# Gate products of a recurrent layer as one fp32 matmul, with a new transfer model in the kernel's order generator

## The chip, the cores and the metric

The program runs on one core of a Trainium2 chip. The metric is device microseconds (us) of one execution of the whole program; the time given for a kernel is the median of several runs. One further execution was recorded by the hardware profiler, and all durations, waits and idle times below come from that record.

The core has four compute engines with a queue of instructions each, and each queue is worked off in order: PE (matrix products), DVE (vector work), ACT (activation functions and copies) and POOL (general work). SP is the fifth queue; here it issues all DMA transfers. An engine whose next instruction has to wait holds everything behind it.

## The reference

Two layers over a sequence of 2048 frames of width 1024, batch 1, all in fp32. Layer 0 is a recurrent block, layer 1 a gated delta rule. Cut to what the change touches, layer 0 is

```
cond = silu(c) @ ada_w + ada_b                     # shift, scale, gate of each layer
h    = rmsnorm(x) * (1 + scale) + shift
xb, zg = split(h @ in_w)                           # 1024 -> 2 x 1024
xf   = causal_conv4(xb) + conv_b
pre  = einsum('bsni,knij->kbsnj', xf, gate_w)      # 2 gates, 8 blocks of 128 x 128
r, i = sigmoid(pre + gate_b)
a    = exp(-8 * r * softplus(-lam))
hseq = scan(a, sqrt(1 - a*a) * (i * xf))           # linear recurrence over time
x    = x + gate * ((hseq * silu(zg)) @ out_w)
```

The line `pre` holds the gate products. Layer 1 projects to q, k, v, z and two small columns, convolves, runs the delta rule in chunks for 8 heads of 128, and projects back; a final rmsnorm follows.

## The kernel before, in words

Time runs along the free dimension in tiles of 128 partitions by 512 columns. The sequence is done in two halves (`u`, 1024 frames each) of two tiles (`i`). PE's main work are the projections ("mm" for the input projections, "mmo" for the output projections, both at line 696): every fp32 operand is split into a high and a low part of the rounded type fp32r, and each product is three matmuls, high by high, low by high and high by low. The splits cost a cast and a subtraction on ACT, DVE or POOL.

The stages follow one another: the conditioning vector (0 to 60 us); the input projection of layer 0 with convolution, gates and scan (about 60 to 500); its output projection out1 with the normalisation and transposition of what layer 1 reads (500 to 700); the projections and heads of layer 1 (700 to 1700, and some of it later); out2 and the final norm (to 1914).

The gates of layer 0: `conv1_thread` produces xf (three multiply-adds on DVE at line 786, which read the product from PSUM, and a few small steps that end at line 799). `gates_thread` makes its high part xh (ACT, line 828) and its low part xl (DVE, line 831). `lru_thread` loads the gate weights gw and splits them into gh (ACT, line 902) and gl (POOL, line 905). For each of the two gates three matmuls follow (line 837), then `gate_thread` applies the activation. `z1_thread` makes the gate path tz (ACT line 813, DVE line 815). The normalised input of the second half is split into hh and hl by `split_thread` (DVE lines 596 and 598), after it was stored transposed and loaded again (xt_d, stored at line 537, loaded as xk at line 573). In out1, `y_thread` loads yf (line 951) and splits it into yh (ACT, line 955) and yl (DVE, line 959).

No order of instructions is written out. Threads (Python generators) ask for an engine and a duration, `Weave` plays them against its own clock and writes the instructions down in the order in which it reaches them. So every number in a `yield`, and every rule in `Weave.transfer`, sets the order on all five queues; it does not change what an instruction costs. `transfer` says when a planned transfer has landed; `MARGIN` is a reserve behind landings: a thread that uses loaded data waits a half or the whole of it (in the plan alone) before it asks for an engine. On the chip, the semaphores between the engines make every instruction wait for what it really needs.

Of the kernel before, what the change touches and what calls it, by code (L numbers as in the profile page):

```python
# [16 lines left out]
P = 128  # L17
# [3 lines left out]
TC = 512  # L21
# [11 lines left out]
MARGIN = 2.4  # L33
# [7 lines left out]
LANDS = {"sp": 1.375, "st": 1.07}  # L41
# [32 lines left out]
class Weave:  # L74
    def __init__(self):
# [3 lines left out]
        self.landed = [0.0] * 8  # L79
# [21 lines left out]
    def start(self, th):  # L101
# [9 lines left out]
        if w[0] in LANDS:  # L111
            return max(th.t, self.free["sp"], self.landed[-8])
# [17 lines left out]
    def transfer(self, th, t, kind, dur, wait=True):  # L130

        self.free["sp"] = t + 0.45
        self.free["dma"] = max(t + 1.04, self.free["dma"]) + dur
        self.landed.append(self.free["dma"] + LANDS[kind])
        th.t = self.landed[-1] + 0.05 if wait else t + 0.45

    def run(self):
        while self.threads:
# [15 lines left out]
            elif w[0] in LANDS:  # L154
# [9 lines left out]
def trunk_kernel(ctx, tc, x, head, small, ada_w, ada_b, final_g, w1, gate_w, ow1, w2, wab, ow2, out):  # L164
# [17 lines left out]
    def f(ap):  # L182
        return ap.bitcast(F32)
# [45 lines left out]
    tags |= {t: ("l1", n) for t, n in {"xh": 2, "xf1": 2, "tg": 4, "th": 2, "tz": 2, "gw": 1, "gh": 1, "gl": 1, "head": 1}.items()}  # L229
# [79 lines left out]
    def first_loads_thread():  # L309

        yield ev("firstpanel")
        for half in range(2):
# [19 lines left out]
    def first_small_thread():  # L332
        yield "sp", 0.29, False
        sp.dma_start(out=head_s, in_=head)
        w.spawn(arrive_thread(ev("head")), 0)
        yield "sp", 0.29, False
# [82 lines left out]
    def row_halves_thread(parts):  # L419
# [3 lines left out]
        for layer, part, d in parts:  # L423
            ttok = yield slots["tt"]
            acc = tile_([P, TC], "tt", "acc")
            for q in range(4):
                wtok = yield slots["raw"]
                yield "sp", 1.4
# [27 lines left out]
            yield "sp", 1  # L456
# [6 lines left out]
            if layer == 1:  # L463
                yield "st", 0.29
# [60 lines left out]
    def turn_thread(key, t_d, xt, tok, ttok, b):  # L525
        yield from scale_thread(xt, ev("scaled", key, b), True)
        for d in range(2):
# [7 lines left out]
            for c_ in range(4):  # L535
                yield "st", 0.31, c_ == 3
# [86 lines left out]
    def panel_load(name, p):  # L623
# [3 lines left out]
        yield "sp", 1.4, False  # L627
# [5 lines left out]
    def panels_thread():  # L633
        yield ev("small")
        ahead = []
        for name, panels, _ in plans:
            for m, p in enumerate(panels):
# [23 lines left out]
                if name[1] > 0:  # L661

                    kept = yield ev("kept", p)
                    yield "sp", 1.4, False
# [18 lines left out]
    def keep_thread(p, lo):  # L683
        kept = dram.tile([P, KT, P], F32, name=f"wlo_d{p[0]}{p[1]}{p[2]}")
        yield "st", 1.4
# [133 lines left out]
    def gates_thread(u, n, i):  # L819
        xf, ftok = yield ev("xf", u, n, i)  # L820
        gh, gl = yield ev("gw", u, n)
        etok = yield slots["xh"]
        ltok = yield slots["xr"]
        if (u, n, i) == (NU - 1, KT - 1, NTC - 1):
            w.set(ev("lasthalves"))
        yield "act", 0.521
        xh = tile_([P, TC], "xh", "xh", F32R)
        act.copy(xh, xf)
        yield "dve2", 0.599
        xl = tile_([P, TC], "xr", "xl", F32R)  # L830
        dve.tensor_tensor(xl, xf, f(xh), ALU.subtract)
        for g in range(2):
            ctok = yield slots["c"]
            yield "pe", 0.696
            pg = ps.tile([P, TC], F32, tag="c", name="pg")
            for q, (a, b) in enumerate(((gh, xh), (gh, xl), (gl, xh))):
                pe.matmul(pg, lhsT=a[:, g, :], rhs=b, start=(q == 0), stop=(q == 2))
            w.spawn(gate_thread(u, n, i, g, pg, ctok), 3)
        put("xh", etok)
        put("xr", ltok)  # L840
# [36 lines left out]
        yield "st", 1  # L877
# [13 lines left out]
    def lru_thread():  # L891
        for u in range(NU):
            for n in range(KT):
                wtok = yield slots["gw"]
                yield "sp", 0.48
                gw = tile_([P, 2, P], "gw", "gw")
                sp.dma_start(out=gw, in_=gate_w[n])
                htok = yield slots["gh"]
                ltok = yield slots["gl"]
                yield "act", 0.302  # L900
                gh = tile_([P, 2, P], "gh", "gh", F32R)
# [901 lines left out]
```

## Time and profile before

| | us |
|---|---|
| median of 3 runs | 1911.61 |
| the runs | 1911.36 to 1918.54 |
| profiled execution, its own time | 1915.63 |
| span in its record, first to last instruction | 1913.9 |
| mean granted TensorE clock | 0.988 of full speed |

In the views, "busy" of PE is counted from modelled ends of pipelined matmuls: two matmuls that follow each other at 0.23 us are drawn 0.39 us long each. What a matmul costs in a stream is therefore the distance from its start to the next start. "Idle before" and the waits are gaps in which PE had nothing in flight. A wait is written as "engine line it stood at <- what ended the wait".

### The profile page before, as it was taken

The page shows a single profiled execution, that of the slowest core. Times are in us where ns is not written, and L with a number is a line of the kernel's source. Part 1 is how long each engine was busy: PE and PEld are TensorE (multiplying, and loading weights), DVE is VectorE, ACT ScalarE, POOL GpSimd, SP SyncE. Part 2 cuts the span into 40 slices and gives each one's busy share as a digit, 9 for nine tenths or more (in the row PEclk, how much of TensorE's full clock was granted, in tenths as well). Part 3 has the DMA queues.
Part 4 walks back from the last instruction along what each step waited for, and adds up shares of the span by engine and source line. Part 5 has one row for each costly group of instructions (what it writes and reads, how often), then busy time and mean ns, then how long its engine had stood idle before and what let it go on. Part 6 is the DMA issues. An engine that isn't in the chain of part 4 may idle for free.

```text
span 1913.9 us, 31154 instructions
## 1 busy us (share of the span) xinstructions
PE 1834.6 (96%) x10286; PEld 1492.7 (78%) x10286; DVE 1366.0 (71%) x3153; ACT 1183.9 (62%) x2749; POOL 382.1 (20%) x912
## 2 busy tenths in 40 slices
PE   6999898999999899999999999999999999999998
PEld 4777676888777678788788887787887877888887
DVE  7888977878644557768788876667676667767653
ACT  4666667777211348786787775677877668754221
POOL 1121210111000014133123321132232122211010
PEclk9999999999999899999999999999999999999999
DMA  8475736544688634557676667266554546587851
GB/s 345 123 219 156 239 121 205 170 160 158 220 207 217 207 92 143 152 134 182 162 183 179 145 149 216 73 164 153 123 149 117 148 129 155 138 219 220 252 154 67
DMA packets 510427, 322.77 MB, mean 169 GB/s; under 512 B 369844, under 2 KB 437940, under 8 KB 510264
## 3 DMA queue, kind: packets, MB, share of 16 engines
q1 hardware_dynamic: 510264, 320.77, 60.0%
q8 instruction: 81, 1.33, 0.3%
q14 instruction: 82, 0.67, 0.1%
HBM read 219.93 MB, written 100.73 MB: 168 GB/s over the span
## 4 chain that ended last, share of the span: by engine, by line
PE 35%; DVE 7%; DMA 6%; ACT 6%; SPq 3%; issue 2%; POOL 1%; DVEq 0%; POOLq 0%; ACTq 0%
PE mm L696 17%; PE mmo L696 9%; DVE xf L748 2%; DMA raw<-in_w 2%; PE py L1446 1%; PE pp L1429 1%; PE pS L1459 1%; PE pS L1458 1%; PE pp L1430 1%; SPq L1245 1%; DVE ttmp L1309 1%; DVE tblk L1312 1%; DMA oraw<-in_ow 1%; ACT junk L1163 1%; PE pkk L1186 1%
## 5 line engine op out<-in xcount | busy, mean ns | idle before, releaser
L748 DVE SCALAR_TENSOR_TENSOR xf<-xe,small_s,xf 128x512 f32<-128x512 f32 x288 | 214.6, 749 | 38.8 <-ACT xf L1027 34.2
L672 ACT CAST whi<-raw 128x1024 fp32r<-128x1024 f32 x96 | 100.2, 1044 | 47.8 <-DMA raw<-in_w 41.1
L1309 DVE TENSOR_TENSOR ttmp<-blk,tblk 128x60 f32<-128x60 f32 (+24 forms) x496 | 104.2, 210 | 29.6 <-DMA blk<-blk_d 6.6
L1312 DVE TENSOR_TENSOR tblk<-tblk,ttmp 128x60 f32<-128x60 f32 (+24 forms) x496 | 107.8, 217 | 12.1
L696 PE MATMUL mmo<-oh,yh 128*128 128x512 f32 x256 | 102.2, 399 | 8.0 <-ACT yh L955 8.0
L696 PE MATMUL mm<-hh_('in2', 0)_5289,whi 128*128 128x512 f32 x256 | 104.0, 406 | 4.5 <-ACT tz L1042 4.5
L696 PE MATMUL mm<-hh_('in2', 1)_12167,whi 128*128 128x512 f32 x256 | 104.3, 408 | 0.7 <-ACT xe L760 0.7
L696 PE MATMUL mm<-hh_('in2', 1)_11901,whi 128*128 128x512 f32 x256 | 105.0, 410 | 0.0
L696 PE MATMUL mm<-hl_('in2', 1)_12168,whi 128*128 128x512 f32 x256 | 104.7, 409 | 0.0
L696 PE MATMUL mm<-hh_('in2', 1)_12167,wlo 128*128 128x512 f32 x256 | 104.7, 409 | 0.0
L696 PE MATMUL mmo<-oh,yl 128*128 128x512 f32 x256 | 103.2, 403 | 1.4 <-DVE yl L959 1.3
L696 PE MATMUL mm<-hh_('in2', 1)_11901,wlo 128*128 128x512 f32 x256 | 104.0, 406 | 0.0
L696 PE MATMUL mm<-hl_('in2', 0)_5290,whi 128*128 128x512 f32 x256 | 103.7, 405 | 0.0
L696 PE MATMUL mm<-hh_('in2', 0)_5435,wlo 128*128 128x512 f32 x256 | 103.4, 404 | 0.0
L696 PE MATMUL mm<-hl_('in2', 1)_11902,whi 128*128 128x512 f32 x256 | 103.3, 403 | 0.0
L696 PE MATMUL mm<-hh_('in2', 0)_5289,wlo 128*128 128x512 f32 x256 | 103.1, 403 | 0.0
L696 PE MATMUL mmo<-oh,ol 128*128 128x512 f32 (+1 forms) x264 | 102.7, 389 | 0.0
L696 PE MATMUL mmo<-oh,oh 128*128 128x512 f32 (+1 forms) x264 | 102.7, 389 | 0.0
L696 PE MATMUL mm<-hh_('in2', 0)_5435,whi 128*128 128x512 f32 x256 | 102.5, 400 | 0.0
L696 PE MATMUL mmo<-ol,oh 128*128 128x512 f32 (+1 forms) x264 | 102.4, 388 | 0.0
L696 PE MATMUL mm<-hl_('in2', 0)_5436,whi 128*128 128x512 f32 x256 | 102.2, 399 | 0.0
L763 POOL COPY carry<-xe 128x4 f32<-128x4 f32 x96 | 23.7, 247 | 392.8 <-ACT xe L760 392.2
(322 smaller groups left out, 5549.6 us busy)
## 6 DMA issues: line engine op xcount, KB each, us to landing
raw<-in_w SPq DMA_DIRECT2D x96, 512.0 KB, 4.5
araw<-in_ada_w SPq DMA_DIRECT2D x32, 512.0 KB, 4.6
xt<-x_d SPq DMA_DIRECT2D x32, 512.0 KB, 5.3
xt_d<-xb SPq DMA_DIRECT2D x192, 64.0 KB, 2.4
xk<-xt_d SPq DMA_DIRECT2D x24, 512.0 KB, 6.4
xt<-in_x SPq DMA_DIRECT2D x16, 512.0 KB, 5.8
ada<-in_ada_w SPq DMA_DIRECT2D x16, 512.0 KB, 10.1
y_d<-tz SPq DMA_DIRECT2D x32, 256.0 KB, 3.5
```

The source lines that it names most:

```text
L672: act.copy(hi, raw)
L696: pe.matmul(pt, lhsT=lhs[a][:, k, :], rhs=rhs[b][:, k, :], start=(k == 0 and n == 0), stop=(k == KT - 1 and n == 2))
L748: dve.scalar_tensor_tensor(xf, xe[:, 1 + j:1 + j + TC], wc[:, j:j + 1], xf, ALU.mult, ALU.add)
L763: pool.tensor_copy(out=carry, in_=xe[:, TC:TC + 4])
L1163: act.activation(junk, kd[:, b, :], AF.Square, accum_out=ss[:, b:b + 1])
L1186: pe.matmul(pkk[:, b, :], lhsT=kc, rhs=kc, start=True, stop=True)
L1245: sp.dma_start(out=dst[r], in_=tb[32 * r:32 * r + 32])
L1309: dve.tensor_tensor(tmp, blk[:, j, j + 1:32].unsqueeze(2).to_broadcast([P, r, c_]), t[:, j, 0:c_].unsqueeze(1).to_broadcast([P, r, c_]), A ...
L1312: dve.tensor_tensor(t[:, j + 1:32, 0:c_], t[:, j + 1:32, 0:c_], tmp, ALU.subtract)
L1429: pe.matmul(pp[:, 0, :], lhsT=kc, rhs=S_, start=True, stop=True)
L1430: pe.matmul(pp[:, 1, :], lhsT=qc, rhs=S_, start=True, stop=True)
L1446: pe.matmul(py, lhsT=rm[:, b, :], rhs=zt, start=True, stop=True)
```

## The change

It has two parts. The first changes the computation of the gate products: xf and the gate weights are no longer split. One fp32 matmul for each gate takes xf and gw as they are, in place of three fp32r matmuls. The casts xh and gh, the subtractions xl and gl, and their buffers go; xf gets three buffers in place of two, gw two in place of one.

The second changes the order generator: transfers pass through one queue (`free["dma"]`) and then, one after the other, through a second stage (`through`); a thread that waits for its store goes on 0.5 us behind the planned landing (before, 0.05), which is when what it stored may be loaded again, and a load keeps 0.05; `MARGIN` goes from 2.4 to 1.0; and the planned durations of the transfers are new (some thirty lines of the kind shown last; the full list differs only in the numbers).

```diff
-MARGIN = 2.4
+MARGIN = 1.0
...
-LANDS = {"sp": 1.375, "st": 1.07}
+TRANSFER = {"sp": (1.56, 0.61, 0.05), "st": (0.74, 0.38, 0.5)}
...
     def transfer(self, th, t, kind, dur, wait=True):
+        front, through, late = TRANSFER[kind]
         self.free["sp"] = t + 0.45
-        self.free["dma"] = max(t + 1.04, self.free["dma"]) + dur
-        self.landed.append(self.free["dma"] + LANDS[kind])
-        th.t = self.landed[-1] + 0.05 if wait else t + 0.45
+        self.free["dma"] = max(t + front, self.free["dma"]) + dur
+        self.through = max(self.free["dma"] + through, self.through + 0.22 + 0.38 * dur)
+        self.landed.append(self.through + 0.46)
+        th.t = self.landed[-1] + late if wait else t + 0.45
...
-    ... {"xh": 2, "xf1": 2, "tg": 4, "th": 2, "tz": 2, "gw": 1, "gh": 1, "gl": 1, "head": 1}
+    ... {"xf1": 3, "tg": 4, "th": 2, "tz": 2, "gw": 2, "head": 1}
...
     def gates_thread(u, n, i):
         xf, ftok = yield ev("xf", u, n, i)
-        gh, gl = yield ev("gw", u, n)
+        gw = yield ev("gw", u, n)
-        yield "act", 0.521
-        act.copy(xh, xf)
-        yield "dve2", 0.599
-        dve.tensor_tensor(xl, xf, f(xh), ALU.subtract)
         for g in range(2):
-            yield "pe", 0.696
+            yield "pe", 0.86
-            for q, (a, b) in enumerate(((gh, xh), (gh, xl), (gl, xh))):
-                pe.matmul(pg, lhsT=a[:, g, :], rhs=b, start=(q == 0), stop=(q == 2))
+            pe.matmul(pg, lhsT=gw[:, g, :], rhs=xf, start=True, stop=True)
...
     def lru_thread():
-                act.copy(gh, gw)
-                pool.tensor_tensor(gl, gw, f(gh), ALU.subtract)
...
-        yield "sp", 1.4, False        # the load of a weight panel, as an example
+        yield "sp", 1.3, False
-                yield "st", 0.31, c_ == 3     # a quarter of a transposed store
+                yield "st", 0.53, c_ == 3
```

How the order moves is shown at three places. The first is PE at the first gates of layer 0, between the products "mm" of a projection. Before:

```order
L696 MATMUL mm<-hh_('in1', 0)_475,whi 128x512
L837 MATMUL pg<-xh,gh 128x512
L837 MATMUL pg<-xl,gh 128x512
L837 MATMUL pg<-xh,gl 128x512
L696 MATMUL mm<-hl_('in1', 0)_476,whi 128x512
L837 MATMUL pg<-xh,gh 128x512
L837 MATMUL pg<-xl,gh 128x512
L837 MATMUL pg<-xh,gl 128x512
L696 MATMUL mm<-hh_('in1', 0)_475,wlo 128x512
```

Now:

```order
L698 MATMUL mm<-hh_('in1', 0)_466,wlo 128x512
L830 MATMUL pg<-xf_453,gw 128x512
L698 MATMUL mm<-hh_('in1', 0)_466,whi 128x512
L830 MATMUL pg<-xf_453,gw 128x512
L698 MATMUL mm<-hl_('in1', 0)_467,whi 128x512
```

Six matmuls for the two gates of a tile have become two, at the same place of the projection.

The second place is DVE where the input of the second half is split (hh, hl) between the end of the first half and the start of the second, some 230 us into the program. Before, after the three multiply-adds of two convolutions, which are not shown:

```order
L799 TENSOR_SCALAR xf_2009<-xf_2009,small_s 128x3
L864 TENSOR_TENSOR tg<-tg 128x512
L596 CAST hh_('in1', 1)_2023<-h 128x512 x2
L598 TENSOR_TENSOR hl_('in1', 1)_2024<-h,hh_('in1', 1)_2023 128x512 x2
L868 SCALAR_TENSOR_TENSOR tg<-th,hcar,tg 128x512
L596 CAST hh_('in1', 1)_2023<-h 128x512 x2
L598 TENSOR_TENSOR hl_('in1', 1)_2024<-h,hh_('in1', 1)_2023 128x512 x2
L875 TENSOR_TENSOR tz<-tz,tg 128x512
L596 CAST hh_('in1', 1)_2023<-h 128x512
L831 TENSOR_TENSOR xl<-xf_1990,xh 128x512
```

Now, from the second split on:

```order
L598 CAST hh_('in1', 1)_1778<-h 128x512
L788 SCALAR_TENSOR_TENSOR xf_1853<-mm,small_s,xf_1853 128x509
L600 TENSOR_TENSOR hl_('in1', 1)_1779<-h,hh_('in1', 1)_1778 128x512
L598 CAST hh_('in1', 1)_1778<-h 128x512
L788 SCALAR_TENSOR_TENSOR xf_1853<-mm,small_s,xf_1853 128x509
L600 TENSOR_TENSOR hl_('in1', 1)_1779<-h,hh_('in1', 1)_1778 128x512
L598 CAST hh_('in1', 1)_1778<-h 128x512
L680 TENSOR_TENSOR wlo<-raw_1801,whi 128x1024
```

Before, the splits stood between finished convolutions and the xl that PE needed next; now there is no xl, and the splits stand between the multiply-adds of a convolution.

The third place is SP at the end of out1 (yf: the last input of out1; xk: the transposed input of layer 1, loaded again; xr and x_d: residual in and out). Before:

```order
L573 DMA xk<-xt_d 128x2x512 x3
L989 DMA x_d<-xr 128x512
L573 DMA xk<-xt_d 128x2x512
L951 DMA yf<-y_d 128x8x128
L573 DMA xk<-xt_d 128x2x512
L989 DMA x_d<-xr 128x512
```

Now:

```order
L932 DMA yf<-y_d 128x8x128
L970 DMA x_d<-xr 128x512
L575 DMA xk<-xt_d 128x2x512 x4
L970 DMA x_d<-xr 128x512
L981 DMA xr<-in_x 128x512
```

The last yf stood behind four loads of xk; now it stands ahead of the first.

More of the change, by code (lines that the diff above doesn't have):

```diff
@@ L78, in __init__ @@
         self.table = "exp"
-        self.landed = [0.0] * 8
+        self.landed, self.through = [0.0] * 8, 0.0
         self.threads = []
@@ L153, in run @@
                 value, w.taken = w.taken, w.taken + 1
-            elif w[0] in LANDS:
+            elif w[0] in TRANSFER:
                 self.transfer(th, t, *w)
@@ L228, in trunk_kernel @@
     tags |= {t: ("ps", 2) for t in ("mm", "tp", "c", "d")}
-    tags |= {t: ("l1", n) for t, n in {"xh": 2, "xf1": 2, "tg": 4, "th": 2, "tz": 2, "gw": 1, "gh": 1, "gl": 1, "head": 1}.items()}
+    tags |= {t: ("l1", n) for t, n in {"xf1": 3, "tg": 4, "th": 2, "tz": 2, "gw": 2, "head": 1}.items()}
     tags |= {"edge1": ("l1", 1)}
@@ L332, in first_small_thread @@
     def first_small_thread():
-        yield "sp", 0.29, False
+        yield "sp", 0.23, False
         sp.dma_start(out=head_s, in_=head)
         w.spawn(arrive_thread(ev("head")), 0)
-        yield "sp", 0.29, False
+        yield "sp", 0.23, False
         sp.dma_start(out=small_s, in_=small)
@@ L455, in row_halves_thread @@
                 n = 1
-            yield "sp", 1
+            yield "sp", 0.84
             j = 2 * part + d
@@ L626, in panel_load @@
         rtok = yield slots["raw"]
-        yield "sp", 1.4, False
+        yield "sp", 1.3, False
         raw = tile_([P, KT, P], "raw", f"raw{n}")
@@ L876, in gates_thread @@
         put("tg", itok)
-        yield "st", 1
+        yield "st", 1.1
         t0 = u * T + i * TC
@@ L894, in lru_thread @@
                 wtok = yield slots["gw"]
-                yield "sp", 0.48
+                yield "sp", 0.33
                 gw = tile_([P, 2, P], "gw", "gw")
                 sp.dma_start(out=gw, in_=gate_w[n])
[L898 to L901, printed above, removed]
-                act.copy(gh, gw)
-                yield "pool2", 1.02
-                gl = tile_([P, 2, P], "gl", "gl", F32R)
-                pool.tensor_tensor(gl, gw, f(gh), ALU.subtract)
-                put("gw", wtok)
-                w.set(ev("gw", u, n), (gh, gl))
+                w.set(ev("gw", u, n), gw)
                 for i in range(NTC):
@@ L911, in lru_thread @@
                     yield ev("gated", u, n, i)
-                put("gh", htok)
-                put("gl", ltok)
+                put("gw", wtok)
     def out_weights_thread(key, src, d, scale, slot, before, after):
@@ L948, in y_thread @@
             tok = yield slots["yf"]
-            yield "sp", 1.4
+            yield "sp", 1.3
             yf = tile_([P, KT, P], "yf", "yf")
@@ L987, in residual1_thread @@
         put(bank, mtok)
-        yield "st", 1
+        yield "st", 0.84
         sp.dma_start(out=x1_d[b * P:(b + 1) * P, d * TC:(d + 1) * TC], in_=xr)
@@ L997, in xr_thread @@
             xtok = yield slots["xr"]
-            yield "sp", 1
+            yield "sp", 0.84
             xr = tile_([P, TC], "xr", "xr")
@@ L1051, in decay_thread @@
         ttok = yield slots["tt"]
-        yield "sp", 0.29
+        yield "sp", 0.23
         wraw = tile_([P, KT, 16], "tt", "wabr")
@@ L1135, in key_thread @@
         etok = yield slots["ec"]
-        yield "sp", 1.2
+        yield "sp", 0.92
         ec = tile_([P, TB, P], "ec", "ec")
@@ L1197, in key_thread @@
         for b in range(4):
-            yield "st", 0.078, b == 3
+            yield "st", 0.13, b == 3
             q0 = b * NB + i * TB
@@ L1215, in norm_q_thread @@
         htok = yield slots["hf"]
-        yield "sp", 1.2
+        yield "sp", 0.92
         pq = tile_([P, TB, P], "hf", "pq")
@@ L1255, in value_thread @@
         ntk = yield slots["vn"]
-        yield "sp", 1.2
+        yield "sp", 0.92
         vn = tile_([P, TB, P], "vn", "vn")
@@ L1330, in levels_thread @@
             for b in range(4):
-                yield "sp", 0.078, i == NTC - 1 and b == 3
+                yield "sp", 0.016, i == NTC - 1 and b == 3
                 q0 = b * NB + i * TB
@@ L1570, in o_loads_thread @@
             tok = yield slots["b4"]
-            yield "sp", 1.4, False
+            yield "sp", 1.3, False
             on = tile_([P, KT, P], "b4", "on")
@@ L1574, in o_loads_thread @@
             ztok = yield slots["b4"]
-            yield "sp", 1.4, False
+            yield "sp", 1.3, False
             zs = tile_([P, KT, P], "b4", "zs")
@@ L1687, in rows_thread @@
         for name, src in (("g2", gate_d), ("fg", final_g)):
-            yield "sp", 1.4
+            yield "sp", 1.3
             row = tile_([P, D], name, name)
```

30 lines of the change are left out of this document (12 added, 18 removed).

## The prediction

> **What bounds the kernel now.** I read the page first, then the busy time by stage, then what PE waited for in each stage, then the timeline at the longest waits. The page's span and its row for PE:
>
> ```profile
> span 1913.9 us, 31154 instructions
> PE 1834.6 (96%) x10286; PEld 1492.7 (78%) x10286; DVE 1366.0 (71%) x3153; ACT 1183.9 (62%) x2749; POOL 382.1 (20%) x912
> ```
>
> The busy time of the engines by stage (columns: stretch, its length, PE, weight loads, DVE, ACT, POOL, granted clock, DMA share, GB/s):
>
> ```profile
> 0.00:60.00 60.00, 44.40 (x182) 29.59 (x182) 46.09 (x108) 28.13 (x46) 11.49 (x30) 0.97 0.70 276
> 60.00:500.00 440.00, 419.56 (x1805) 338.74 (x1805) 367.75 (x603) 301.47 (x427) 72.97 (x95) 0.98 0.59 181
> 500.00:700.00 200.00, 189.47 (x801) 148.32 (x800) 98.66 (x164) 44.60 (x61) 8.34 (x25) 0.97 0.66 184
> 700.00:1700.00 1000.00, 975.42 (x6458) 807.11 (x6457) 732.47 (x2122) 743.15 (x2063) 266.33 (x700) 0.99 0.60 152
> 1700.00:1914.00 214.00, 205.77 (x1047) 168.94 (x1045) 120.98 (x159) 66.55 (x153) 22.97 (x62) 0.99 0.59 178
> ```
>
> PE bounds every stage but the first. The time is PE's work, plus the gaps in which PE has nothing to do, plus what a lowered clock adds behind a gap. The gaps are 440 - 419.6 = 20.4 us in layer 0, 10.5 in out1, 24.6 in layer 1. These 55 us and the clock are all that a new order can win; a change of PE's work counts in full. What PE waited for in layer 0 (60 to 500 us), then in out1 (500 to 700), then the largest in layer 1 (700 to 1700); columns: total, times, longest:
>
> ```profile
> PE mm L696 <- DVE xf L786: 10.0, 6, 3.2
> PE pg L837 <- DVE xl L831: 5.1, 3, 4.4
> PE mm L696 <- DVE tz L815: 3.8, 2, 2.0
> ...
> PE mmo L696 <- ACT yh L955: 8.0, 3, 6.3
> ...
> PE mm L696 <- ACT tz L1042: 4.5, 2, 3.8
> ```
>
> In layer 0 it is DVE that comes late; in out1 it is the split of yf.
>
> **The change part by part.**
>
> *PE's work rises by 10.9 us.* Three gate matmuls of before, and the one after them:
>
> ```profile
> 124.21 0.39 PE L837 MATMUL pg<-xh,gh 128*128 128x512 f32 x1
> 124.44 0.40 PE L837 MATMUL pg<-xl,gh 128*128 128x512 f32 x1
> 124.67 0.39 PE L837 MATMUL pg<-xh,gl 128*128 128x512 f32 x1
> 124.90 0.39 PE L837 MATMUL pg<-xh,gh 128*128 128x512 f32 x1
> ```
>
> From start to start a gate takes 124.90 - 124.21 = 0.69. An fp32 matmul of the same shape stands in the stream in one place of layer 0, as the conditioning product adapt, two records long:
>
> ```profile
> 150.96 1.02 PE L448 MATMUL adapt<-acc,ones 128*128 128x512 f32 x2
> 151.42 0.79 PE L837 MATMUL pg<-xh,gh 128*128 128x512 f32 x1
> 152.05 0.39 PE L837 MATMUL pg<-xl,gh 128*128 128x512 f32 x1
> ```
>
> From 150.96 to 152.05 are 1.09 us for adapt and one gate matmul of 0.23, so 0.86 for adapt. There are 64 gates (2 halves, 8 blocks, 2 tiles, 2 gates): 64 x (0.86 - 0.69) = +10.9. Nothing covers it, since PE bounds the stage.
>
> The Trainium skill, "FP8 and Floating Point Precision", section "TensorE Precision Notes", states that a true fp32 product takes four passes through the array, which speaks against this change. Four passes at this trace's 0.23 would be 0.92, an estimate, and the term +14.7; the trace agrees that it is more than three passes, and gives 0.86.
>
> *DVE, ACT and POOL lose the splits.* By line, in 60 to 500 us (busy, mean ns, idle before):
>
> ```profile
> L831 DVE TENSOR_TENSOR xl<-xf,xh 128x512 fp32r<-128x512 f32 x32 | 23.3, 736 | 3.8 <-ACT xh L828 3.4
> L828 ACT CAST xh<-xf 128x512 fp32r<-128x512 f32 x32 | 19.8, 618 | 46.6 <-DVE xf L799 46.3
> L905 POOL TENSOR_TENSOR gl<-gw,gh 128x256 fp32r<-128x256 f32 x15 | 13.9, 926 | 50.4 <-ACT gh L902 50.4
> ```
>
> ACT (301 of 440 busy) and POOL (73) are not what PE waits for, so their share is worth nothing directly. DVE goes from 368 to 345 us in a stage that becomes some 5 us shorter or longer: from 84% to about 78%.
>
> *The wait for xl goes: -5.1.* There is no xl. Next in line is xf's last step, line 799; the order rows of before show eight rows of DVE between that step and an xl, so xf was ready long before, and I take the whole 5.1. The bounds are 0 (a new lateness of xf takes its place) and -5.1.
>
> *The waits for xf and tz halve: -6.9.* They are 13.8 us, and the bounds are 0 and -13.8. DVE's load falls, but the order now sets eight pairs of splits between the multiply-adds of a convolution, so that PSUM comes free later just there. Neither end is nearer, so I take the middle.
>
> *The clock behind those gaps: -3.5.* The longest gaps by the timeline (start, length drawn, then in brackets the gap before it):
>
> ```profile
> 233.10 0.79 PE L837 MATMUL pg<-xl,gh 128*128 128x512 f32 x1 [4.38 <-DVE xl L831]
> 267.11 0.75 PE L696 MATMUL mm<-hh_('in1', 1)_2023,whi 128*128 128x512 f32 x1 [2.03 <-DVE tz L815]
> 650.41 0.80 PE L696 MATMUL mmo<-oh,yh 128*128 128x512 f32 x1 [6.29 <-ACT yh L955]
> ```
>
> The busy time in a stretch around each of the three; the granted clock follows the column of POOL:
>
> ```profile
> 230.00:250.00 20.00, 15.12 (x48) 11.71 (x49) 16.75 (x30) 15.91 (x23) 7.97 (x4) 0.74 0.43 148
> 264.00:274.00 10.00, 7.97 (x28) 6.07 (x27) 9.29 (x16) 5.35 (x9) 0.81 (x2) 0.83 0.35 111
> 648.00:664.00 16.00, 13.38 (x46) 10.30 (x47) 10.58 (x19) 6.34 (x9) 0.00 (x0) 0.74 0.56 195
> ```
>
> A clock of 0.74 over 20 us loses 5.2 us, 0.83 over 10 us loses 1.7; together 6.9, and I take half, with the waits.
>
> The Trainium skill, "TensorE: Matmul & The Clock Gate", section "HAM oscillation — how this bites in real kernels", says that PE should have no idle gap above about 3.4 us. By it a 4.38 gap that is only cut to half gives its whole 5.2 back, and the term would be -5.2 or more; the 2.03 gap with a clock of 0.83 does not agree with that bound.
>
> *Layer 0 in sum:* 10.9 - 5.1 - 6.9 - 3.5 = -4.6.
>
> *Out1: -8.* SP's queue and ACT at the longest wait:
>
> ```profile
> 636.01 1.46 SPq L573 DMA_DIRECT2D xk<-xt_d  x3
> 638.57 0.41 SPq L951 DMA_DIRECT2D yf<-y_d  x1
> 649.33 1.03 ACT L955 CAST yh<-yf 128x1024 fp32r<-128x1024 f32 x1
> ```
>
> The last yf was issued behind four xk of 512 KB and its cast began 10.8 us later. In the new order it stands ahead of all xk, so most of that queueing goes. At stake are the waits of 8.0 and, behind the longest, 16 x 0.26 = 4.2 of clock: 0 to -12.2. What is late next are the other yf loads, which share the stage with the same small transposed stores as before. I take -8, nearer to the full sum because the order answers this one wait directly.
>
> *Layer 1: 0, between -24.6 and +38.* Here only the plan moved. What the smaller reserve touches are the consumers of loads, above all the cast whi of a weight panel on ACT; its waits in 700 to 1700 us, SP's longest wait for a store that is loaded again, and the landing time of a panel:
>
> ```profile
> ACT whi L672 <- DMA raw<-in_w: 20.9, 18, 3.4
> ...
> SPq L1218 <- DMA q_d<-tb: 19.8, 19, 4.8
> ...
> raw<-in_w SPq DMA_DIRECT2D x96, 512.0 KB, 4.5
> ```
>
> Before, the plan put the cast 1.04 + 1.4 + 1.375 + 0.05 + 1.2 = 5.07 us behind the issue of an undisturbed load; now 1.56 + 1.3 + 0.61 + 0.46 + 0.05 + 0.5 = 4.48, against a measured median of 4.5. So ACT will stand at this cast more often: 64 panels by up to 0.6 us are 38 us of waiting on ACT, the upper end. The other way, SP no longer reaches a reload 1 us too early (19.8 us in 19 times), since the plan now lets such a store land later; the lower end is that all gaps of PE go. The nearest row is the first: 20.9 us of waits on ACT that PE did not feel, as its waits in this stage name tz, xe and the heads but not whi. So I take 0.
>
> *First stage and out2: 0.* SP's first 20 transfers and its last 40 stand in the same order as before.
>
> **The sum:** -4.6 - 8 + 0 = -12.6 on the profiled execution, 1915.6 to 1903.0. That execution was 4.0 us above the median of the runs, so I take the same difference from the median: 1911.6 - 12.6 = 1899.
>
> **The rivals.**
>
> *The passes are paid and the waits come back.* DVE's splits now delay xf where xl was late, and another yf is late in out1. For it: 13.8 of layer 0's waits are for xf and tz, not for xl. Against it: DVE's load falls by 23 us. The time: 1911.6 + 10.9 - 5.1 = 1917, between 1908 and 1921.
>
> *Slower: the thin reserve reaches PE in layer 1.* ACT stands at whi, and behind it in its queue stand the small steps of the heads (the scaled copies that PE's next matmul needs). For it: the 4.48 against 4.5. Against it: the 20.9 us that stayed hidden. It decides when the added wait of a panel outlasts the projection matmuls that PE has in reserve. If three quarters of the 38 us come through: 1899 + 28 = 1927, between 1921 and 1937.
>
> *Layer 1 gains too.* With reloads no longer issued too early, half of the 24.6 us and some clock go: 1899 - 14 = 1885, between 1878 and 1890. For it: SP's 19.8 us. Against it: PE's gaps there are many and short, mostly within the heads.
>
> By the skill's four passes, 3.8 us more than in my sum, the forecast would be 1903; that lies inside its range.
>
> **How the numbers follow.** 0.5% of 1911.6, about what a measurement of this kernel can tell from no change, is 9.6 us, so faster means below 1902 and slower above 1921. Forecast 0.45 (own range 1890 to 1907), waits come back 0.22, thin reserve 0.20, layer 1 gains 0.13. Faster: three quarters and a little more of the forecast, and all of the last, 0.35 + 0.13 = 0.48. Same: the rest of the forecast and nearly all of the first rival, 0.10 + 0.19 = 0.29. Slower: 0.20 + 0.03 = 0.23. The range 1880 to 1929 leaves out about half of the slower rival and the far end of the gain. The time is the forecast's.
>
> **What would show it.** PE's gate matmuls 0.86 apart; no wait of PE for xl, and waits for xf and tz together near 7 us in layer 0; a DVE share near 78% there; no wait of 6 us for yh at the end of out1. The prediction is wrong if PE's gaps in layer 1 grow well beyond 25 us, if whi appears among PE's releasers, or if a gap above 4 us stands where the splits of the second half are.

## The result, and the profile after

The changed kernel took 1887.03 us (median of 5 runs, 1882.15 to 1887.59), against 1911.61 before: a ratio of 0.9853, 95% interval 0.9835 to 0.9871. On another chip, beside it, the same kernel gave 0.9857 (0.9834 to 0.9879). The ratio is taken over all runs of both and is not the quotient of the two medians, which is 0.9871: it stands for some 28 us, the medians for 24.6. The direction was forecast, and the time lies in the wide range; but the forecast gain was 12.6 us, and the measured one is about twice that by the medians and more by the ratio.

The page of the kernel after:

```profile
span 1881.1 us, 30918 instructions
PE 1834.2 (98%) x10222; PEld 1473.4 (78%) x10222; DVE 1349.6 (72%) x3121; ACT 1175.6 (62%) x2709; POOL 347.7 (18%) x896
```

PE is busy for as long as before (1834.6); what went is idle time. (Busy time also holds what a low clock adds, so equal sums do not mean equal work.) The busy time by the prediction's stages, after:

```profile
0.00:60.00 60.00, 44.65 (x188) 29.98 (x189) 46.09 (x110) 28.80 (x47) 9.94 (x29) 0.97 0.70 276
60.00:500.00 440.00, 438.57 (x1809) 336.66 (x1808) 355.35 (x582) 288.38 (x386) 53.09 (x80) 1.00 0.61 190
500.00:700.00 200.00, 197.06 (x865) 158.10 (x864) 105.08 (x171) 66.31 (x111) 15.89 (x43) 0.98 0.66 187
700.00:1700.00 1000.00, 981.79 (x6573) 806.56 (x6572) 743.24 (x2133) 742.98 (x2050) 248.51 (x690) 1.00 0.61 156
```

In the 440 us from 60 to 500 (in the changed kernel the last 39 of them belong to out1) PE now stands still for 1.4 us in place of 20.4, and the granted clock is 1.00 in place of 0.98. What PE waited for, in 60 to 500 us and then in 500 to 700:

```profile
PE pg L830 <- DVE xf L801: 1.3, 3, 0.8
...
PE pgc L1085 <- DVE gg L1080: 2.8, 1, 2.8
```

These are all of PE's waits in the two stretches. The waits for xl, for xf and tz (as readers of PSUM) and for yh are gone. The 2.8 us stand at 670 us, in layer 1, which now begins before 700.

The stages do not begin at the same time in the two kernels, so I compare their ends by PE's products: the last gate product, the last product of out1 (`mmo<-oh,yl`), the last of out2 (`mmo<-oh,ol`). The timeline of PE's products, grouped by tile, shows them (count, shortest/median/longest in ns, then first and last start in the stretch asked for). Before:

```profile
L837 PE MATMUL pg<-xh,gl x8: 388/391/397, 441.6 to 483.0; 128*128 128x512 f32 x8
...
L696 PE MATMUL mmo<-oh,yl x87: 389/389/792, 599.9 to 669.8; 128*128 128x512 f32 x87
...
L696 PE MATMUL mmo<-oh,ol x104: 279/392/404, 1840.0 to 1906.5; 128*128 128x512 f32 x88, 128*128 128x256 f32 x16
```

After:

```profile
L830 PE MATMUL pg<-xf,gw x8: 592/592/592, 443.9 to 460.8; 128*128 128x512 f32 x8
...
L698 PE MATMUL mmo<-oh,yl x53: 389/389/398, 600.0 to 635.7; 128*128 128x512 f32 x53
...
L698 PE MATMUL mmo<-oh,ol x57: 279/392/404, 1840.1 to 1873.8; 128*128 128x512 f32 x41, 128*128 128x256 f32 x16
```

| stage | before | after | difference |
|---|---|---|---|
| to the last gate product | 483.0 | 460.8 | -22.2 |
| from there to the end of out1 | 186.8 | 174.9 | -11.9 |
| layer 1 and out2 | 1236.7 | 1238.1 | +1.4 |

The whole gain lies in layer 0 and out1. Layer 1, where only the order changed, gained nothing. The border between the first two rows is not a clean one: some of out1's products already run ahead of the last gate product, 34 before and 10 after (`mmo`, counted in the trace). The difference of 24 products at 0.23 is 5.5 us, which the first row counts as gain and the second as loss. Both rows together, 34.1, are free of this. All three rows sum to 32.7 us, more than the 24.6 between the medians, since the profiled execution of before was 4.0 above its median and that of after (1882.95) 4.1 below its own.

### The profile page after: what moved, and what is told of

Its sections match the earlier page's. It is cut to its first block, busy times and chain, and to the rows that moved or that the text cites. A ratio compares the mean times of both kernels' runs of the same rounds, so it can differ in the third digit from the quotient of the medians.

```text
span 1881.1 us, 30918 instructions
## 1 busy us (share of the span) xinstructions
PE 1834.2 (98%) x10222; PEld 1473.4 (78%) x10222; DVE 1349.6 (72%) x3121; ACT 1175.6 (62%) x2709; POOL 347.7 (18%) x896
## 4 chain that ended last, share of the span: by engine, by line
PE 67%; DVE 12%; DMA 9%; ACT 5%; SPq 4%; issue 2%; POOL 1%; DVEq 0%; POOLq 0%; ACTq 0%
PE mm L698 36%; PE mmo L698 16%; PE pg L830 3%; DMA raw<-in_w 3%; DVE xf L750 2%; DVE ttmp L1290 2%; DVE tblk L1293 2%; PE py L1427 1%; PE pp L1410 1%; PE pS L1440 1%; PE pS L1439 1%; PE pp L1411 1%; DMA oraw<-in_ow 1%; SPq L1226 1%; PE pkk L1167 1%
## 5 line engine op out<-in xcount | busy, mean ns | idle before, releaser
L1293 DVE TENSOR_TENSOR tblk<-tblk,ttmp 128x60 f32<-128x60 f32 (+24 forms) x496 | 106.2, 214 | 12.6
L698 PE MATMUL mm<-hh_('in2', 1)_11657,wlo 128*128 128x512 f32 x256 | 105.1, 410 | 0.0
L698 PE MATMUL mm<-hh_('in2', 0)_4992,whi 128*128 128x512 f32 x256 | 104.1, 407 | 0.7 <-ACT tz L1023 0.7
L698 PE MATMUL mm<-hh_('in2', 1)_11864,wlo 128*128 128x512 f32 x256 | 104.6, 409 | 0.0
L698 PE MATMUL mm<-hl_('in2', 0)_4993,whi 128*128 128x512 f32 x256 | 104.6, 409 | 0.0
L698 PE MATMUL mm<-hh_('in2', 0)_5107,whi 128*128 128x512 f32 x256 | 103.8, 405 | 0.7 <-ACT tz L1023 0.7
L698 PE MATMUL mm<-hl_('in2', 1)_11658,whi 128*128 128x512 f32 x256 | 104.2, 407 | 0.0
L698 PE MATMUL mm<-hh_('in2', 1)_11657,whi 128*128 128x512 f32 x256 | 104.0, 406 | 0.0
L698 PE MATMUL mm<-hl_('in2', 0)_5108,whi 128*128 128x512 f32 x256 | 103.7, 405 | 0.0
L698 PE MATMUL mm<-hh_('in2', 0)_4992,wlo 128*128 128x512 f32 x256 | 103.6, 405 | 0.0
L698 PE MATMUL mm<-hh_('in2', 1)_11864,whi 128*128 128x512 f32 x256 | 103.4, 404 | 0.0
```

The lines of the kernel that those rows point to most:

```text
L698: pe.matmul(pt, lhsT=lhs[a][:, k, :], rhs=rhs[b][:, k, :], start=(k == 0 and n == 0), stop=(k == KT - 1 and n == 2))
L1293: dve.tensor_tensor(t[:, j + 1:32, 0:c_], t[:, j + 1:32, 0:c_], tmp, ALU.subtract)
```

## The experiments

Eighteen more runs were made, one of them the changed kernel again. The questions were which of the two parts brings which stage's gain; why layer 0's waits went entirely; and whether the reserve does anything in layer 1. The table has all runs; "waits" are PE's in 60 to 490 us, the next three columns are the stage ends and lengths as above, in one profiled execution each. A ratio compares a kernel with runs of the kernel before on the same chip; the chips differ (medians of before from 1909 to 1913), so times of a few us apart in different rows are better compared by their ratios. The last gate product moves by some us with how many of out1's products run ahead of it. "Old" and "new" are the transfer model of before and of the change, with the reserve (`MARGIN`) behind it.

| kernel | gates | xf buffers | order | time | ratio to before (95%) | waits | last gate | out1 | layer 1, out2 |
|---|---|---|---|---|---|---|---|---|---|
| before | split | 2 | old 2.4 | 1911.61 | | 20.5 | 483.0 | 186.8 | 1236.7 |
| old_nudge | split | 2 | old 2.0 | 1896.00 | 0.9915 (0.9884, 0.9946) | 18.7 | 477.2 | 183.2 | 1227.0 |
| plan_only | split | 2 | new 1.0 | 1904.17 | 0.9967 (0.9946, 0.9988) | 19.2 | 477.5 | 172.5 | 1239.7 |
| xh_one | split | 2 | new 1.0 | 1899.83 | 0.9945 (0.9921, 0.9969) | 15.1 | 476.2 | 171.7 | 1237.3 |
| plan_16 | split | 2 | new 1.6 | 1912.40 | 1.0010 (0.9996, 1.0024) | 22.3 | 484.2 | 171.3 | 1246.1 |
| xf_three_old | split | 3 | old 2.4 | 1889.57 | 0.9886 (0.9845, 0.9927) | 9.7 | 466.0 | 172.4 | 1243.0 |
| best_old | split | 3 | old 2.0 | 1884.91 | 0.9866 (0.9826, 0.9906) | 12.1 | 465.2 | 180.0 | 1225.7 |
| xf_three | split | 3 | new 1.0 | 1882.49 | 0.9842 (0.9805, 0.9879) | 4.9 | 457.5 | 173.8 | 1244.3 |
| xf_three_16 | split | 3 | new 1.6 | 1874.59 | 0.9816 (0.9772, 0.9860) | 6.0 | 461.2 | 173.8 | 1231.1 |
| xf_three_20 | split | 3 | new 2.0 | 1882.81 | 0.9859 (0.9845, 0.9874) | 12.9 | 475.1 | 173.1 | 1224.8 |
| gates_two_old | one fp32 | 2 | old 2.4 | 1895.34 | 0.9928 (0.9913, 0.9943) | 3.8 | 469.0 | 173.1 | 1243.4 |
| xf_two | one fp32 | 2 | new 1.0 | 1885.71 | 0.9858 (0.9817, 0.9899) | 3.8 | 467.2 | 172.2 | 1239.2 |
| gates_only | one fp32 | 3 | old 2.4 | 1894.35 | 0.9924 (0.9891, 0.9957) | 2.8 | 463.9 | 179.8 | 1242.3 |
| after | one fp32 | 3 | new 1.0 | 1887.03 | 0.9853 (0.9835, 0.9871) | 1.3 | 460.8 | 174.9 | 1238.1 |
| after_again | one fp32 | 3 | new 1.0 | 1882.97 | 0.9857 (0.9834, 0.9879) | 2.2 | 463.1 | 174.5 | 1232.4 |
| after_16 | one fp32 | 3 | new 1.6 | 1877.39 | 0.9836 (0.9819, 0.9852) | 2.4 | 462.8 | 174.6 | 1230.6 |
| after_20 | one fp32 | 3 | new 2.0 | 1878.35 | 0.9826 (0.9804, 0.9848) | 2.0 | 464.7 | 174.5 | 1225.5 |
| margin_24 | one fp32 | 3 | new 2.4 | 1888.52 | 0.9887 (0.9840, 0.9933) | 2.1 | 462.3 | 174.8 | 1240.8 |
| splits_kept | one fp32, splits made | 3 | new 1.0 | 1911.36 | 1.0008 (0.9992, 1.0024) | 4.2 | 468.4 | 173.4 | 1259.7 |
| gates_twice | fp32, twice | 3 | new 1.0 | 1939.04 | 1.0140 (1.0109, 1.0172) | 1.9 | 516.8 | 175.7 | 1236.0 |

### Each part alone, and the reserve put back

gates_only is the kernel before with the new gates and their buffers; plan_only is the new generator with the gates of before; margin_24 is the changed kernel with

```diff
-MARGIN = 1.0
+MARGIN = 2.4
```

> The new gate matmuls with the old order generator (old transfer model, MARGIN 2.4). Theory A (the gate change frees DVE, and that ends layer 0's waits; out1's waits end by the new plan): +10.9 for the passes, -19 of waits and -7 of clock in layer 0, out1 as before with about 10 us of waits for yh and yl: 1897. Theory B (the new plan does both, the gate change only costs): waits for xf and tz stay near 14 us, 1911.6 + 10.9 - 5 = 1917.

> The new order generator with the old gates (three fp32r matmuls, xh, xl, gh, gl made and read). Theory A: out1's 10 us of waits and its clock go, layer 0 keeps some 20 us of waits: about 1894. Theory B: layer 0's waits go too except those for xl, and the passes are not paid: 1887 - 10.9 + 5 = 1881, the fastest of all.

> The changed kernel with MARGIN 2.4 in place of 1.0. If the reserve of 1.0 is what matters, some of the gain in out1 or layer 1 goes, above 1895. If the transfer model matters and the reserve does not, 1887 within 5. A third theory, that any new order draws anew from a wide spread, would show as a change of 10 us or more with waits at places that have nothing to do with loads.

The gates alone end layer 0's waits (2.8 us left, last gate at 463.9). The generator alone leaves them at 19.2, yet brings out1 to 172.5; but the gates alone shorten out1 as well, to 179.8. To the end of out1 the gates alone gain 26.1 us on the profiled executions, the generator alone 19.8, both together 34.1: the two overlap. PE's waits in 60 to 490 us with the generator alone:

```profile
PE pg L839 <- ACT xh L830: 9.5, 2, 8.2
PE mm L698 <- ACT whi L674: 6.5, 1, 6.5
PE pg L839 <- DVE xl L833: 3.2, 3, 2.1
```

Other names than in before, where PE stood at xf, xl and tz, but the same sum. So the names in that list depend on the order, and taking the names out of it one by one, as the prediction did, is not safe. In the whole program the gates alone came near the lower of the two times expected for them (1894.35), the generator alone above both of its own (1904.17). The reserve put back to 2.4 changes neither layer 0 nor out1.

### Is it DVE's load?

The prediction's reason for fewer waits was that DVE loses the splits. In splits_kept the changed kernel still makes xh and xl, which nothing reads (the halves of the weights are not made):

```diff
+        yield "act", 0.521
+        act.copy(xh, xf)
+        yield "dve2", 0.599
+        dve.tensor_tensor(xl, xf, f(xh), ALU.subtract)
         for g in range(2):
```

> The changed kernel, but xh and xl are still made on ACT and DVE and nobody reads them (gh and gl are not made); the plan counts them. It has the fp32 gate matmul without a wait for xl, and the DVE load of before. Theory A (load): the waits for xf and tz in layer 0 come back, 14 us and some clock, about 1905. Theory B (plan): layer 0 stays without waits, 1887 within 4.

The busy time in 60 to 490 us of this kernel:

```profile
60.00:490.00 430.00, 425.84 (x1744) 325.55 (x1743) 361.09 (x602) 290.63 (x408) 56.01 (x80) 1.00 0.59 183
```

DVE is busy for 361 of 430 us, 84%, the share that the prediction read in before; and PE stands still for 4.2 us only. So with three buffers for xf the load of the splits on DVE does not by itself make PE wait. It doesn't follow that DVE's load had no part in before. DVE worked without a break while PE waited there. Four of PE's longer waits, in the columns of the prediction's stages (PE, weight loads, DVE and so on):

```profile
194.30:197.30 3.00, 0.00 (x0) 0.00 (x0) 3.00 (x5) 1.59 (x3) 0.88 (x3) 1.00 0.41 160
228.80:233.00 4.20, 0.00 (x0) 0.00 (x0) 4.20 (x9) 2.18 (x3) 3.29 (x1) 1.00 0.89 339
265.20:267.00 1.80, 0.00 (x0) 0.00 (x0) 1.80 (x4) 1.80 (x4) 0.18 (x1) 1.00 0.65 241
293.90:295.90 2.00, 0.00 (x0) 0.00 (x0) 2.00 (x4) 1.97 (x4) 0.00 (x0) 1.00 0.35 131
```

Over all of PE's waits in 60 to 490 us of before, DVE is busy for 20.1 of 20.4 us. So PE stood behind work that had piled up on DVE. splits_kept has the load of the splits, but it also has the third buffer, which may let DVE take up that work earlier. A kernel with unsplit gates, the load of the splits and two buffers was not run, so load and chain are not separated for two buffers.

The time of the whole, 1911.36, fits neither theory: layer 1 takes 1259.7 us here, the longest of all, though nothing in its code differs. PE stands still for 34.2 of 1260 us there, and for 22.9 of 1238 in the changed kernel; and the granted clock is 0.94 to 0.98 from 642 to 1400 us, which is some 28 us lost against some 8 (an estimate from the rows of 158 to 200 us). Why this order has more gaps and a lower clock stays open.

### Is it the third buffer for xf?

The change also gives xf three buffers in place of two, which the prediction shows in the diff and does not price. xf_two takes the third away from the changed kernel; xf_three gives it to the gates of before, under the new generator; xf_three_old is the kernel before with nothing else changed:

```diff
-    ... {"xh": 2, "xf1": 2, "tg": 4, ...
+    ... {"xh": 1, "xf1": 3, "tg": 4, ...
```

> The changed kernel with two buffers for xf in place of three. Theory A, the third buffer of xf ended layer 0's waits: the matmuls of the first product and the gate product wait for xf and tz again, 10 to 20 us in the stretch from 60 to 490 us, some of it behind a lower clock, the last gate product ends 10 to 20 us later than the 460.8 us of the changed kernel, and the time is near 1900. Theory B, the shorter chain to a gate product (no split, one matmul) ended them: under 4 us of waits in that stretch, the last gate product ends at 459 to 465 us, and the time is near 1887.

> The old gates on split tiles under the new generator, with three buffers for xf (and one for xh, to make room). Theory A (the third buffer): layer 0's 19 us of waits with two buffers fall to under 5, the last gate product ends near 465 us, and the time is 1890. Theory B (the split chain itself): gate products still wait for xh and xl, 8 to 20 us in the stretch from 60 to 490 us, the last gate product ends at 474 to 480 us, and the time is 1902 to 1906.

> The kernel before with one number changed for another: three buffers for xf and one for xh (2 and 2 before); old gates, old generator. Theory A, the third buffer by itself frees layer 0: under 6 us of waits of PE in the stretch from 60 to 490 us, last gate product at 456 to 468 us (482.7 before), time 1886 to 1897. Theory B, it needs the new generator's order too: 12 us of waits or more, last gate product after 475 us, time above 1902.

> The kernel before with its generator's margin set to 2.0, so that its order is another one of the same kind. Theory A, the waits of layer 0 and of out1 belong to the old chains: again 20 to 30 us of waits in the stretch from 60 to 490 us, last gate product at 478 to 487 us, time 1905 to 1918. Theory B, they were an accident of one order: the waits go or move, and the last gate product ends at under 472 us or past 492; the time may be anything from 1890 to 1930.

xf_two says that the unsplit gates are enough, with 3.8 us of waits (its last gate, at 467.2, came 2 us later than either theory's range for a free layer 0; 24 of out1's products run ahead of it, 10 in the changed kernel); xf_three says that the third buffer nearly is, with 4.9, and it runs as fast as the change (0.9842) with the split gates still in place. The kernel before gains 1.1% by this one line, though nearly half of what it gains up to the end of out1 (14.4 of 31.4 us on the profiled executions) lies in out1, which has no xf, and comes from the new order. PE's waits in 60 to 490 us of xf_three:

```profile
PE pg L839 <- DVE xl L833: 2.4, 5, 0.9
PE mm L698 <- ACT whi L674: 1.7, 1, 1.7
PE mm L698 <- DVE wlo L680: 0.6, 1, 0.6
PE adapt L450 <- DVE acc L439: 0.2, 1, 0.2
```

PE stands at xl no less often than in before, but never longer than 0.9 us. Since two different things end the same waits, single orders had to be told from a rule. old_nudge is before with a reserve of 2.0: its layer 0 waits nearly as before (18.7 us, last gate at 477.2, both just under what the first theory gave), so the waits are no accident of one order. Not all of them stand at the gates, though: the longest, 8.6 us, is at adapt, which waits for DVE's acc, and DVE is busy without a break through it. old_nudge is 0.8% faster all the same, a time that this theory did not have: 9.7 us of that lie in layer 1.

### Controls

xh_one has the one xh of xf_three, but two xf. xf_three_16 and plan_16 are xf_three and plan_only with a reserve of 1.6; gates_two_old is gates_only with two xf; best_old is xf_three_old with a reserve of 2.0.

> The control to the old gates with three buffers for xf: old gates, new generator, two buffers for xf and one for xh. Theory A, xf's buffers decide: the 19 us of waits of layer 0 stay, last gate product at 472 to 486 us, time 1900 to 1910. Theory B, any redrawn order may free layer 0: under 6 us of waits, last gate product before 465 us, time 1880 to 1890.

> The kernel before with three buffers for xf, one for xh and a margin of 2.0. Theory A, the two gains add, since the one lies in layer 0 and the other behind it: 1896 less 15 to 20, 1876 to 1881. Theory B, the order behind layer 0 is drawn anew whenever layer 0 changes, and the gain of the margin there is lost: 1886 to 1900.

> Old gates, new generator, three buffers for xf and one for xh, with a margin of 1.6 in place of 1.0. Theory A, layer 0's gain holds in any order: last gate product at 455 to 463 us, under 6 us of waits, time 1876 to 1890. Theory B, it was one lucky order: last gate product after 468 us, time above 1892.

> The unsplit gates under the old generator, with two buffers for xf in place of three. Theory A, leaving the splits out frees layer 0 by itself, since a tile of xf is then held for some 20 us in place of 23 to 26: last gate product at 460 to 469 us, under 5 us of waits in the stretch from 60 to 490 us, time 1888 to 1900. Theory B, the one run with unsplit gates and two buffers was a lucky order: last gate product after 474 us, 10 us of waits or more, time above 1902.

> Old gates, new generator, two buffers for xf and xh, margin 1.6: a fifth order with split gates and two buffers. Theory A, this pair keeps layer 0's waits in any order: last gate product at 474 to 484 us, 12 us of waits or more, time 1893 to 1907. Theory B, the four orders so far were unlucky: last gate product before 468 us, under 6 us of waits, time under 1890.

With split gates and two xf, five orders wait for 15.1 to 22.3 us. With the unsplit gates, every order waits for 4.2 or less, with two xf (two orders) or three. With split gates and three xf, five orders give 4.9 to 12.9: the buffer helps in each of the four that have a partner with two, and frees layer 0 in some. So the third buffer was expected to do too much twice: under 6 us of waits in xf_three_old (9.7 came), and the last gate at 455 to 466 us in xf_three_20 below (475.1); xf_three_16, with 6.0, stands at its border. plan_16 kept the waits, and was slower (1912.40) than either theory had it. best_old came to 1884.91, between its two expectations: layer 1 kept its gain (1225.7), layer 0 gained only 12.

One thing goes with the unsplit gates in every run: the weights are not split either, and gw has two buffers. No run takes this apart from xf's splits. What speaks against it as the cause is that none of PE's waits in the five orders ends with gh or gl.

Where a tile of xf stands can be seen on ACT, whose first step of a convolution takes a free buffer. ACT's waits at that step in before, 60 to 500 us, then in after:

```profile
ACT xf L776 <- DVE tg L857: 14.5, 9, 2.7
```

```profile
ACT xf L778 <- PE mm L698: 61.4, 21, 4.6
```

Before, a convolution waits nine times for the last reader of xf (`tg`, line 857), that is, for a buffer; after, it only waits for PE's product. From the start of the first step to the end of the last reader, averaged over the 32 tiles, xf is held for 26.0 us in before and 18.3 in after, and a new tile comes every 13.6 and 13.1 us: 1.9 of two buffers in use, then 1.4 of three. This fits the buffer as a link between the split chain and PE's waits. It isn't the only one, and in plan_only it is none: with split gates and two buffers, ACT never waits for a buffer at this step, only for PE's product.

```profile
ACT xf L778 <- PE mm L698: 55.3, 22, 4.6
```

plan_only holds xf for 20.6 us, no longer than gates_two_old, and still waits for 19.2, half of it at a late xh; xf_three_20 holds it for 20.7 with three buffers and waits for 12.9. What is shown is which kernels wait and which don't; by which link was not separated.

### PE's work

gates_twice issues each gate product a second time:

```diff
-            pe.matmul(pg, lhsT=gw[:, g, :], rhs=xf, start=True, stop=True)
+            for _ in range(2):
+                pe.matmul(pg, lhsT=gw[:, g, :], rhs=xf, start=True, stop=True)
```

> The changed kernel with each gate product issued twice, and planned so; what the second writes is the same product again. Theory A, PE sets the end of layer 0 with next to no slack: 64 more matmuls of 0.86 count in full, +55, the time is 1937 to 1947 and the last gate product ends at 511 to 521 us. Theory B, part of the gate products lies in time in which PE would have waited: under +40, below 1927.

64 more gates cost 56.0 us at the last gate product (516.8 against 460.8), 55 expected; so each counts in full, at 0.88. Three lines of PE's timeline in the changed kernel show the same (start, length drawn):

```profile
111.45 1.02 PE L830 MATMUL pg<-xf,gw 128*128 128x512 f32 x2
111.91 0.80 PE L698 MATMUL mm<-hh_('in1', 0)_226,whi 128*128 128x512 f32 x1
112.54 0.40 PE L698 MATMUL mm<-hl_('in1', 0)_227,whi 128*128 128x512 f32 x1
```

From 111.45 to 112.54 are 1.09, less one product at 0.23: 0.86, as adapt had shown before.

### The reserve in layer 1

> The changed kernel with a margin of 1.6 in place of 1.0. Layer 1 and out2 (from the last product of out1 to the last of out2) took 1231 us in the run with this margin on split gates with three xf, 1226 and 1227 in the two runs with 2.0 and the old transfer model, and 1236 to 1244 in nearly all others. Theory A, a reserve between the two is worth about 8 us there: 1226 to 1233, time 1876 to 1881. Theory B, those three are the spread of orders: 1236 to 1244, time 1883 to 1890.

> Old gates, new generator, three buffers for xf, one for xh, margin 2.0. Theory A, the reserve counts in layer 1: from out1's end to the last product 1225 to 1233 us, time 1870 to 1879. Theory B, spread: 1236 to 1244, time 1880 to 1890. In layer 0 both expect the last gate product at 455 to 466 us, as with three buffers before.

> The changed kernel with a margin of 2.0 in place of 1.0. From out1's end to the last product, the three runs with 2.0 took 1225 to 1227 us (1230 to 1246 with 1.6, 1236 to 1260 with 1.0, 1237 to 1243 with 2.4). Theory A, the reserve sets layer 1's time: 1224 to 1229 us, out1's end stays at 635 to 642, the time is 1870 to 1876, 8 us or more below the changed kernel. Theory B, those three are chance: 1235 to 1244 us there, time 1881 to 1890.

> The changed kernel as it is, on the same chip as the run with a margin of 2.0, to compare the two. Theory A: 8 us or more above that run; theory B: within 5 us of it. Both expect 1882 to 1889.

The last column of the table, by reserve: 2.4 gives 1237 to 1243 (5 orders), 2.0 gives 1225 to 1227 (4), 1.6 gives 1231, 1231 and 1246, and 1.0 gives 1232 to 1244 (7 executions) and once 1260. Four of four with 2.0 are the four shortest, with either gates and either transfer model, so the value counts: some 7 to 13 us in profiled executions. PE stands still in this stretch for 18.4 us in after_20 and 22.9 in the changed kernel. The change goes from one side of the best of these values to the other, which fits that layer 1 shows nothing; by what the value acts is open. In the times it is less: after_20 took 1878.35 (1873.95 to 1879.68) beside 1882.97 (1880.09 to 1884.30) for the changed kernel on the same chip, 4.6 us where 8 or more were expected, which is what the second theory of after_again had (within 5); the runs of the two don't overlap. xf_three_20, with 1224.8 behind out1, came to 1882.81 all the same, since its layer 0 ended late. The lowest ratios are those of xf_three_16, after_20 and after_16 (0.9816 to 0.9836); all three intervals overlap with the change's, and only after_20 ran beside it.

## Why the prediction was right in direction and short in size

- **PE's passes, +10.9: right.** 0.86 by the timeline; 0.88 by gates_twice. The four passes of the Trainium skill ("FP8 and Floating Point Precision", section "TensorE Precision Notes") made an estimate of 0.92, above both.
- **The wait for xl, -5.1: right in amount.** It is gone, and what came in its place is 1.3 us for xf. (In the order rows the step at line 799 is of another tile, xf_2009, than the xl, of xf_1990; that one was ready earlier still.)
- **"The waits for xf and tz halve", -6.9: this is the step that failed.** All 13.8 us went; with xl and the small ones, 20.5 became 1.3. I took the middle of 0 and -13.8 because two reasons spoke against each other, and neither decided. DVE's share did not fall: up to each kernel's last gate product DVE is busy for 352 of 423 us before and 335 of 401 after, 83 and 84%, and with three buffers the load of the splits leaves PE 4.2 us of waits (splits_kept). The eight pairs of splits between the multiply-adds cost nothing that shows. What I treated as kinds of waits, to be ended one by one, came and went together: with the split in the gate's chain and two buffers for xf, 15 to 22 us stood in all five orders, under changing names; without the split no order had more than 4.2. The third buffer for xf stood in the diff, and the wait for a buffer on ACT (14.5 us in 9 times) in the trace of before; the sum has no term for either.
- **The clock, -3.5 in layer 0: too small, by the same halving.** The stretch from 200 to 270 us, before and then after:

```profile
200.00:270.00 70.00, 61.81 (x245) 48.98 (x244) 63.56 (x111) 48.21 (x70) 14.30 (x11) 0.91 0.62 200
```

```profile
200.00:270.00 70.00, 69.78 (x292) 53.95 (x291) 60.82 (x109) 50.21 (x70) 8.46 (x9) 1.00 0.59 193
```

  A clock of 0.91 over 70 us is 6.3 us, and all of it came back. The rule of the Trainium skill ("TensorE: Matmul & The Clock Gate", section "HAM oscillation — how this bites in real kernels") that the prediction weighed asks for no gaps above about 3.4 us; the longest wait that is left in layer 0 is 0.8, so this row agrees with it.
- **Out1, -8: short.** The stage shrank by 11.9, close to the 12.2 that I had as its end, but partly by chance: it also took in 24 products (5.5 us) that ran in layer 0 before. Its waits lost 10.4, not 8.0, as those for yl and for adapt went too; the clock follows below. The wait for yh went as argued: under the new transfer model 14 profiled executions give 171 to 176 us, under the old one six give 172 to 187. But xf_three_old and gates_two_old have 172.4 and 173.1 with the old model, so a better order was also to be had without it.
- **Layer 1, 0: right in sum.** It was +1.4. One of its two arguments did not hold. SP's wait for q_d, the longest of those for a store that is loaded again, fell from 19.8 to 8.1, but the next, for v_d, rose from 12.1 to 24.6 (first before, 700 to 1700 us, then after, 690 to 1680):

```profile
SPq L1258 <- DMA v_d<-tb: 12.1, 10, 5.7
```

```profile
SPq L1239 <- DMA v_d<-tb: 24.6, 19, 4.7
SPq L1199 <- DMA q_d<-tb: 8.1, 6, 3.8
```

  All of SP's waits for such stores together are 45.1 us before and 43.4 after, so reloads are still issued too early. The other argument held: ACT's waits for a panel rose from 20.9, and whi is not among PE's releasers there:

```profile
ACT whi L674 <- DMA raw<-in_w: 28.4, 21, 4.5
```

  Neither rival came true, at this value of the reserve. That 1887 lies between the bounds of "Layer 1 gains too" (1878 to 1890) is chance: the gain lay in layer 0 and out1.

The sum by measured terms, on the profiled executions: +10.9 for the passes, -19.2 for layer 0's waits, -10.4 for out1's (8.0, 1.3 and 1.1 for another adapt product, now none), +1.4 behind it. To the -32.7 of the stage ends 15.4 are missing. The clock has a part in it: the row above has 6.3. For out1 these rows of before show where it was lowered; after has 1.00 in all of out1:

```profile
598.30:601.70 3.40, 3.21 (x8) 2.54 (x9) 1.78 (x4) 0.00 (x0) 0.00 (x0) 0.50 0.80 194
646.10:650.40 4.30, 0.00 (x0) 0.00 (x0) 4.16 (x9) 3.42 (x5) 0.00 (x0) 0.50 1.05 383
650.50:656.30 5.80, 5.59 (x13) 3.90 (x14) 3.62 (x6) 2.10 (x3) 0.00 (x0) 0.50 0.82 283
```

The second row lies inside the 6.29 us gap, where a lowered clock costs PE nothing. What is left is 3.4 and 5.8 us at one half, 4.6 us. (So the prediction's 4.2 behind this gap, taken over 16 us with part of the gap in them, was too much.) 15.4 - 6.3 - 4.6 leaves 4.5 us that are not accounted for; some of it is work that now runs ahead of 60 us (188 records of PE there, 182 before).

## What to carry to other kernels

Where a bounding engine waits under several names in one stage, look for what they share before halving each: which buffer is full, which chain holds it, and whether the engine that comes late is itself busy without a break. Price every number in the diff, buffer counts too, and ask for each whether it gives by itself what the costly part promises: here one buffer moved from xh to xf brought the old kernel about as much as the new gates did (0.9886 and 0.9924, with intervals that overlap). And try a few orders of each kind before crediting a difference of a per cent to one edit, where a planner redraws the whole program.

## What the runs showed of the hardware

Behind a gap of PE of the same length the clock stayed low for different times. At the start of layer 1 the changed kernel has a wait of 2.8 us, in both of its executions. The 16 us around it show a mean clock of 0.79 in one and of 0.89 in the other:

```profile
668.00:684.00 16.00, 13.18 (x49) 10.76 (x49) 11.67 (x23) 6.74 (x12) 2.85 (x7) 0.79 0.44 137
```

```profile
668.00:684.00 16.00, 13.19 (x54) 10.36 (x53) 12.64 (x30) 7.01 (x13) 1.47 (x5) 0.89 0.36 109
```

Shorter stretches show that the clock fell to one half in both, for some 7 us in the first and half as long in the second (0.21 and 0.11 of 16 us, doubled). The rows, first and then second:

```profile
671.00:677.00 6.00, 6.00 (x18) 4.87 (x19) 4.85 (x7) 3.40 (x7) 0.10 (x1) 0.50 0.25 96
677.20:684.00 6.80, 6.80 (x31) 5.61 (x30) 4.20 (x5) 1.97 (x4) 2.54 (x5) 1.00 0.81 236
```

```profile
675.00:678.00 3.00, 3.00 (x9) 2.32 (x8) 2.72 (x5) 2.29 (x4) 0.10 (x1) 0.50 0.38 134
678.10:684.00 5.90, 5.90 (x27) 4.88 (x26) 3.54 (x4) 2.40 (x4) 1.15 (x3) 1.00 0.72 199
```

So a gap's length does not give its price, and a gap under the bound of about 3.4 us that the prediction cited from the Trainium skill ("TensorE: Matmul & The Clock Gate", section "HAM oscillation — how this bites in real kernels") was followed by a lower clock in both. It fits that layer 1 of this one kernel took 1238.1 us in one execution and 1232.4 in the other: some 6 us are the spread of one order here, and a difference of that size between two single profiles says nothing.
